# Loading b in long runs, restoring its order in ScalarE's writes, and giving PE whole batches in sequence

## The chip, the cores and the metric

The kernel runs on one core of a Trainium2 chip. The metric is the device time of a run in microseconds (us). PE is the matmul engine (PEld its weight loads), VectorE is DVE in the views, ScalarE is ACT, and SP issues the transfers. "PEclk" is the share of PE's full clock that was granted.

## The reference

```python
batch, m, k, n = 16, 512, 512, 512        # a: [16, 512, 512], b: [16, 512, 512], float32
np.matmul(a, b.transpose(0, 2, 1)).astype(np.float32)
```

Per batch both operands are cast to bf16 and turned by PE (32 transposes of 128 x 128), so that k lies on the partitions in both, as the program's matmuls take them. Then 16 matmuls of 128 x 512 columns make four products of 128 x 512. Two inputs and one output of 1 MB each move per batch, 50.33 MB in all.

## The kernel before

```python
def load(i):
    ...
    nc.sync.dma_start(a_sb[:], a[i].rearrange("(p j) k -> p j k", j=J))    # 8 KB runs
    nc.sync.dma_start(b_sb[:], b[i].rearrange("(o p) k -> p o k", p=P))    # 2 KB runs
def halve(i):
    ...
    nc.scalar.copy(out=a_h[:], in_=a_sb[:])            # ScalarE casts a
    nc.vector.tensor_copy(out=b_h[:], in_=b_sb[:])     # VectorE casts b
def turn(i, ko):                                       # 4 transposes of a, 4 of b, one copy
    ...
    nc.vector.tensor_copy(out=turned[i][:, ko, :], in_=tp[:])
def multiply(i, j):                                    # 4 matmuls, one product copied
    ...
    nc.scalar.copy(out=made[i][:, j, :], in_=ps[:])
...
for i in range(batch):
    for s in range(4):
        multiply(i, s)
        ...
        if i + 1 < batch:
            turn(i + 1, s)
    if i + 2 < batch:
        halve(i + 2)
    ...                                                # store(i), load(i + 5)
```

## Time and profile before

| | kernel before |
|---|---|
| time, median of 3 runs | 131.27 us (130.75 to 131.88) |
| span of the profiled run | 129.7 us |
| DMA engines busy | 97.0% |
| PE, VectorE, ScalarE busy | 74%, 49%, 51% |
| mean granted clock of PE | 0.971 |

The prediction below shows the lines that carry this. Start with the DMA row and the chain's shares: they say whether transfers or engines set the end. Then take single durations from the groups, and the pace of a run of matmuls from the chain, because a matmul's own record holds its latency (392 ns on the mean here, at a pace of 215).

### The profile page before, as it was taken

The page shows a single profiled execution, that of the slowest core. Times are in us where ns is not written, and L with a number is a line of the kernel's source. Part 1 is how long each engine was busy: PE and PEld are TensorE (multiplying, and loading weights), DVE is VectorE, ACT ScalarE, POOL GpSimd, SP SyncE. Part 2 cuts the span into 40 slices and gives each one's busy share as a digit, 9 for nine tenths or more (in the row PEclk, how much of TensorE's full clock was granted, in tenths as well). Part 3 has the DMA queues.
Part 4 walks back from the last instruction along what each step waited for, and adds up shares of the span by engine and source line. Part 5 has one row for each costly group of instructions (what it writes and reads, how often), then busy time and mean ns, then how long its engine had stood idle before and what let it go on. Part 6 is the DMA issues. An engine that isn't in the chain of part 4 may idle for free.

```text
span 129.7 us, 1868 instructions
## 1 busy us (share of the span) xinstructions
PE 95.7 (74%) x768; PEld 55.1 (42%) x768; DVE 63.3 (49%) x80; ACT 66.3 (51%) x81; POOL 0.7 (1%) x6
## 2 busy tenths in 40 slices
PE   0018796969696969687795988879594967969930
PEld 0018363636363636253452545445261634535400
DVE  0026746565656656454655265465545545456200
ACT  3225248483838383827454174756447381283530
POOL 2000000000000000000000000000000000000000
PEclk9999999999999999999999599999999997799998
DMA  3999999999999999999999999999999999999592
GB/s 114 361 427 382 405 423 388 414 403 433 385 428 403 420 415 393 433 367 429 410 420 425 400 433 397 419 417 415 430 399 426 397 431 414 415 426 384 245 349 80
DMA packets 13497, 50.46 MB, mean 389 GB/s; under 512 B 816, under 2 KB 816, under 8 KB 9520
## 3 DMA queue, kind: packets, MB, share of 16 engines
q1 hardware_dynamic: 13488, 50.33, 97.0%
q8 instruction: 6, 0.10, 0.3%
q14 instruction: 3, 0.02, 0.1%
HBM read 33.55 MB, written 16.78 MB: 388 GB/s over the span
## 4 chain that ended last, share of the span: by engine, by line
DMA 53%; PE 26%; ACT 8%; DVE 5%; issue 3%; SPq 1%; DVEq 0%; ACTq 0%
DMA b_sb<-in_b_dram 53%; PE ps L81 17%; ACT a_h L58 7%; PE tp L71 5%; PE tp L69 4%; DVE b_h L59 4%; DVE ab_T L72 2%; SPq L50 1%; ACT o_sb L85 1%; SPq L51 0%; DVEq L59 0%; ACTq L85 0%
## 5 line engine op out<-in xcount | busy, mean ns | idle before, releaser
L81 PE MATMUL ps<-ab_T 128*128 128x512 bf16 x256 | 70.6, 392 | 2.2
L72 DVE COPY ab_T<-tp 128x1024 bf16<-128x1024 bf16 x64 | 44.3, 692 | 41.9 <-PE tp L71 41.8
L85 ACT COPY o_sb<-ps 128x512 f32<-128x512 f32 x64 | 37.5, 586 | 50.5 <-PE ps L81 50.5
L69 PE MATMUL tp<-ident,a_h 128*128 128x128 bf16 x256 | 26.4, 229 | 19.4 <-ACT a_h L58 19.4
L69 PEld LDWEIGHTS <-a_h 128*128 128x128 bf16 x256 | 19.6, 103 | 35.5 <-ACT a_h L58 23.6
L58 ACT CAST a_h<-a_sb 128x2048 bf16<-128x2048 f32 x16 | 30.4, 1902 | 7.4 <-DMA a_sb<-in_a_dram 7.4
L81 PEld LDWEIGHTS <-ab_T 128*128 128x128 bf16 x256 | 22.9, 100 | 24.7 <-DVE ab_T L72 10.1
L71 PE MATMUL tp<-ident,b_h 128*128 128x128 bf16 x256 | 26.3, 228 | 7.0 <-DVE b_h L59 6.9
L59 DVE CAST b_h<-b_sb 128x2048 bf16<-128x2048 f32 x16 | 19.6, 1224 | 16.1 <-DMA b_sb<-in_b_dram 16.0
L71 PEld LDWEIGHTS <-b_h 128*128 128x128 bf16 x256 | 17.8, 102 | 8.6 <-DVE b_h L59 8.6
L58 ACT ACT_TABLE_LOAD x1 | 1.3, 1283 | 0.7 <-PEq L127 0.7
masks.py:199 POOL TENSOR_SCALAR_AFFINE_SELECT ident<-ident 128x128 bf16<-128x128 bf16 x1 | 0.3, 292 | 0.1
masks.py:197 POOL MEMSET ident<- 128x128 bf16 x1 | 0.2, 205 | 0.3 <-POOLq L127 0.3
L127 POOL MEMSET const-bfloat16-1.0<- 128x1 bf16 x1 | 0.1, 101 | 0.0
L127 POOL MEMSET const-uint8-127<- 128x1 uint8 x1 | 0.1, 101 | 0.0
L127 POOL MEMSET const-float32-0.0<- 128x1 f32 x1 | 0.1, 98 | 0.2 <-issue 0.2
L127 POOL MEMSET const-float32-1.0<- 128x1 f32 x1 | 0.1, 98 | 0.0
## 6 DMA issues: line engine op xcount, KB each, us to landing
a_sb<-in_a_dram SPq DMA_DIRECT2D x16, 1024.0 KB, 16.9
b_sb<-in_b_dram SPq DMA_DIRECT2D x16, 1024.0 KB, 18.8
out_dram<-o_sb SPq DMA_DIRECT2D x15, 1024.0 KB, 17.5
out_dram<-o_sb SPq DMA_DIRECT2D x4, 256.0 KB, 3.8
```

The costliest lines, as they stand in the source:

```text
L50: nc.sync.dma_start(a_sb[:], a[i].rearrange("(p j) k -> p j k", j=J))
L58: nc.scalar.copy(out=a_h[:], in_=a_sb[:])
L59: nc.vector.tensor_copy(out=b_h[:], in_=b_sb[:])
L69: nc.tensor.transpose(tp[:, j * P:(j + 1) * P], a_h[:, j, ko * P:(ko + 1) * P], ident[:])
L71: nc.tensor.transpose(tp[:, M + o * P:M + (o + 1) * P], b_h[:, o, ko * P:(ko + 1) * P], ident[:])
L72: nc.vector.tensor_copy(out=turned[i][:, ko, :], in_=tp[:])
L81: nc.tensor.matmul(ps[:], ab_T[:, ko, j * P:(j + 1) * P], ab_T[:, ko, M:], start=(ko == 0), stop=(ko == KO - 1),)
L85: nc.scalar.copy(out=made[i][:, j, :], in_=ps[:])
L127: nc = _bacc.Bacc("TRN2", target_bir_lowering=False, num_devices=1)
```

## The change

The intent is to read b in 8 KB runs as well as a. A partition then holds four neighbouring rows of b, so a product's columns come out in a permuted order. ScalarE puts them right as it copies a product out: it writes each 4-byte element 16 bytes after the last. In the same change PE takes a batch whole (a's transposes, b's, the matmuls) instead of alternating between two batches, and VectorE casts both operands. Beside these, the pools of the loads go from 5 to 6 buffers, those of the turned operands from 3 to 2, and the last output is stored whole instead of in four parts.

```diff
-        nc.sync.dma_start(b_sb[:], b[i].rearrange("(o p) k -> p o k", p=P))
+        nc.sync.dma_start(b_sb[:], b[i].rearrange("(p j) k -> p j k", j=J))
 ... (cuts: pools, names, the old halve and turn)
+    def turn(src, tag):
+        half = hpool.tile([P, J, K], bf16, tag="h" + tag)
+        nc.vector.tensor_copy(out=half[:], in_=src[:])
+        turned = tpool.tile([P, KO, J * P], bf16, tag="t" + tag)
+        for ko in range(0, KO, 2):
+            tp = tppool.tile([P, 2, J * P], bf16, tag="tp")
+            ... (eight transposes)
+            nc.vector.tensor_copy(out=turned[:, ko:ko + 2, :], in_=tp[:])
 ...
-        nc.scalar.copy(out=made[i][:, j, :], in_=ps[:])
+            nc.scalar.copy(
+                out=o_sb[:, j, :].rearrange("m (p j) -> m j p", j=J),
+                in_=ps[:].rearrange("m (j p) -> m j p", j=J),
+            )
 ...
+            aT = turn(a_sb, "a")
+            bT = turn(b_sb, "b")
+            o_sb = multiply(aT, bT)
+            store(i, o_sb)
```

More of the change, by code (lines that the diff above doesn't have):

```diff
@@ L22 @@
     J = M // P
-    NO = N // P
     KO = K // P
@@ L31 @@
     make_identity(nc, ident)
-    apool = ctx.enter_context(tc.tile_pool(name="a_pool", bufs=5))
-    bpool = ctx.enter_context(tc.tile_pool(name="b_pool", bufs=5))
+    apool = ctx.enter_context(tc.tile_pool(name="a_pool", bufs=6))
+    bpool = ctx.enter_context(tc.tile_pool(name="b_pool", bufs=6))
     hpool = ctx.enter_context(tc.tile_pool(name="h_pool", bufs=2))
-    tpool = ctx.enter_context(tc.tile_pool(name="t_pool", bufs=3))
+    tpool = ctx.enter_context(tc.tile_pool(name="t_pool", bufs=2))
     opool = ctx.enter_context(tc.tile_pool(name="o_pool", bufs=5))
@@ L39 @@
     ppool = ctx.enter_context(tc.tile_pool(name="p_pool", bufs=4, space=bass.MemoryType.PSUM))
-    loaded = {}
-    halved = {}
-    turned = {}
-    made = {}
     def load(i):
         a_sb = apool.tile([P, J, K], f32, tag="a")
-        b_sb = bpool.tile([P, NO, K], f32, tag="b")
+        b_sb = bpool.tile([P, J, K], f32, tag="b")
         nc.sync.dma_start(a_sb[:], a[i].rearrange("(p j) k -> p j k", j=J))
-        nc.sync.dma_start(b_sb[:], b[i].rearrange("(o p) k -> p o k", p=P))
-        loaded[i] = (a_sb, b_sb)
@@ L54, in halve @@
-    def halve(i):
-        a_sb, b_sb = loaded[i]
-        a_h = hpool.tile([P, J, K], bf16, tag="ah")
-        b_h = hpool.tile([P, NO, K], bf16, tag="bh")
-        nc.scalar.copy(out=a_h[:], in_=a_sb[:])
-        nc.vector.tensor_copy(out=b_h[:], in_=b_sb[:])
-        halved[i] = (a_h, b_h)
-    def turn(i, ko):
-        if ko == 0:
-            ab_T = tpool.tile([P, KO, M + N], bf16, tag="t")
-            turned[i] = ab_T
-        a_h, b_h = halved[i]
-        tp = tppool.tile([P, M + N], bf16, tag="tp")
-        for j in range(J):
-            nc.tensor.transpose(tp[:, j * P:(j + 1) * P], a_h[:, j, ko * P:(ko + 1) * P], ident[:])
-        for o in range(NO):
-            nc.tensor.transpose(tp[:, M + o * P:M + (o + 1) * P], b_h[:, o, ko * P:(ko + 1) * P], ident[:])
-        nc.vector.tensor_copy(out=turned[i][:, ko, :], in_=tp[:])
@@ L74, in multiply @@
-    def multiply(i, j):
-        ab_T = turned[i]
-        if j == 0:
-            o_sb = opool.tile([P, J, N], f32, tag="o")
-            made[i] = o_sb
-        ps = ppool.tile([P, N], f32, tag="p")
-        for ko in range(KO):
-            nc.tensor.matmul(
-                ps[:], ab_T[:, ko, j * P:(j + 1) * P], ab_T[:, ko, M:],
-                start=(ko == 0), stop=(ko == KO - 1),
-            )
-        nc.scalar.copy(out=made[i][:, j, :], in_=ps[:])
-    def store(i):
-        nc.sync.dma_start(out[i].rearrange("(p j) n -> p j n", j=J), made[i][:])
@@ L90, in store_part @@
-    def store_part(i, j):
-        nc.sync.dma_start(out[i].rearrange("(p j) n -> p j n", j=J)[:, j, :], made[i][:, j, :])
+        nc.sync.dma_start(b_sb[:], b[i].rearrange("(p j) k -> p j k", j=J))
+        return a_sb, b_sb
+    def turn(src, tag):
[4 more added lines that the diff above has]
+            tp = tppool.tile([P, 2, J * P], bf16, tag="tp")
+            for h in range(2):
+                for j in range(J):
+                    nc.tensor.transpose(
+                        tp[:, h, j * P:(j + 1) * P],
+                        half[:, j, (ko + h) * P:(ko + h + 1) * P],
+                        ident[:],
+                    )
+            nc.vector.tensor_copy(out=turned[:, ko:ko + 2, :], in_=tp[:])
+        return turned
@@ new lines, in multiply @@
+    def multiply(aT, bT):
+        o_sb = opool.tile([P, J, N], f32, tag="o")
+        for j in range(J):
+            ps = ppool.tile([P, N], f32, tag="p")
+            for ko in range(KO):
+                nc.tensor.matmul(
+                    ps[:], aT[:, ko, j * P:(j + 1) * P], bT[:, ko, :],
+                    start=(ko == 0), stop=(ko == KO - 1),
+                )
+            nc.scalar.copy(
+                out=o_sb[:, j, :].rearrange("m (p j) -> m j p", j=J),
+                in_=ps[:].rearrange("m (j p) -> m j p", j=J),
+            )
+        return o_sb
@@ L93, with store @@
+    def store(i, o_sb):
+        nc.sync.dma_start(out[i].rearrange("(p j) n -> p j n", j=J), o_sb[:])
+    loaded = {}
     with tc.manual_schedule():
         for i in range(min(AHEAD, batch)):
-            load(i)
-        halve(0)
-        for s in range(KO):
-            turn(0, s)
-        halve(1)
-        for i in range(batch):
-            for s in range(4):
-                multiply(i, s)
-                if i == batch - 1:
-                    store_part(i, s)
-                if i + 1 < batch:
-                    turn(i + 1, s)
-            if i + 2 < batch:
-                halve(i + 2)
-            if i < batch - 1:
-                store(i)
+            loaded[i] = load(i)
+        for i in range(batch):
+            a_sb, b_sb = loaded.pop(i)
+            aT = turn(a_sb, "a")
+            bT = turn(b_sb, "b")
+            o_sb = multiply(aT, bT)
+            store(i, o_sb)
@@ L111 @@
             if i + AHEAD < batch:
-                load(i + AHEAD)
+                loaded[i + AHEAD] = load(i + AHEAD)
 _INS = ['a', 'b']
```

## The prediction

> **What bounds the kernel now.** I read the page first (shares, slices, queues, chain summary), then the groups, the chain in order of time, and the granted clock over 3.41 us stretches. From the page, the transfer rows:
>
> ```profile
> DMA  3999999999999999999999999999999999999592
> ...
> q1 hardware_dynamic: 13488, 50.33, 97.0%
> ...
> DMA 53%; PE 26%; ACT 8%; DVE 5%; issue 3%; SPq 1%; DVEq 0%; ACTq 0%
> ```
>
> The 16 DMA engines are busy in every slice until the last three, 97% of the span, and transfers are 53% of the chain that ended last. No compute engine is over 74%. So the kernel before is bound by moving 50.33 MB, with little to spare: where the chain is not in DMA it runs on PE at 6.58 us a batch (a's cast ends at 28.18 and again at 34.76), against 3.15 MB / 412 GB/s (mean of 20 to 120 us) = 7.6 us of DMA.
>
> From the groups, the durations that I reuse (busy us, then mean ns of one):
>
> ```profile
> L81 PE MATMUL ps<-ab_T 128*128 128x512 bf16 x256 | 70.6, 392 | 2.2
> L72 DVE COPY ab_T<-tp 128x1024 bf16<-128x1024 bf16 x64 | 44.3, 692 | 41.9 <-PE tp L71 41.8
> L85 ACT COPY o_sb<-ps 128x512 f32<-128x512 f32 x64 | 37.5, 586 | 50.5 <-PE ps L81 50.5
> ...
> L58 ACT CAST a_h<-a_sb 128x2048 bf16<-128x2048 f32 x16 | 30.4, 1902 | 7.4 <-DMA a_sb<-in_a_dram 7.4
> ...
> L59 DVE CAST b_h<-b_sb 128x2048 bf16<-128x2048 f32 x16 | 19.6, 1224 | 16.1 <-DMA b_sb<-in_b_dram 16.0
> ```
>
> The 392 ns of a matmul is pipelined latency; the pace is read from the chain (start, us, what):
>
> ```profile
> 116.03 0.05 issue
> 116.08 0.40 PE tp L69 x4
> 116.47 0.22 PE tp L71 x4
> 116.70 0.86 PE ps L81 x4
> ...
> 120.67 0.70 DVE ab_T L72
> 121.37 0.05 issue
> 121.41 2.99 PE ps L81 x13
> 124.43 0.58 ACT o_sb L85
> ```
>
> Four matmuls cost 0.86 us (0.215 each), four transposes 0.22 (0.40 for the first four after a wait), a hand-over between engines about 0.05. In the kernel before these hand-overs lie beside other work, because PE alternates four matmuls of batch i with eight transposes of batch i+1.
>
> The clock matters too (us, PE busy and count, PEld, DVE, ACT, POOL, PEclk, DMA share, GB/s):
>
> ```profile
> 9.62:13.03 3.41, 2.93 (x28) 2.94 (x29) 2.38 (x4) 1.70 (x1) 0.00 (x0) 1.00 0.99 383
> ...
> 67.64:71.06 3.42, 1.69 (x13) 0.77 (x13) 1.78 (x3) 2.03 (x2) 0.00 (x0) 1.00 1.02 432
> 71.06:74.47 3.41, 3.41 (x16) 1.76 (x15) 1.13 (x2) 0.58 (x1) 0.00 (x0) 0.50 1.01 393
> 98.36:101.78 3.42, 1.83 (x17) 1.06 (x17) 1.92 (x2) 1.42 (x3) 0.00 (x0) 1.00 1.01 422
> 105.19:108.60 3.41, 1.60 (x13) 0.76 (x12) 1.69 (x3) 2.08 (x2) 0.00 (x0) 1.00 1.01 425
> 108.60:112.02 3.42, 3.42 (x16) 1.77 (x14) 1.27 (x2) 0.58 (x1) 0.00 (x0) 0.50 1.01 398
> ```
>
> A stretch with too little PE work is followed by one at half clock. Counting by starts, 67.64 holds 4 matmuls and 8 transposes (3072 columns), 105.19 holds 3 and 8 (2560): both are followed by half clock. 98.36 holds 4 and 12 (3584 columns) and is not. At 2.4 columns per ns the limit lies between 1.28 and 1.49 us of column time in 3.41 us; I take 1.4.
>
> [...] the stretch from 9.62 holds 28 transposes and no matmul, and full clock was granted at its end (the 1.00 printed for that stretch itself precedes the first clock record). [...] the trace's busy slices show 367 to 433. [...]
>
> **The change part by part.**
>
> *b in 8 KB runs.* The packet records have 309 ns for 8192 bytes and 84 ns (median) for 2048. Per 8 KB that saves 4 x 84 - 309 = 27 ns; 2048 such runs over 16 engines give 3.5 us in all. It is a gain only while DMA binds.
>
> *Casts.* ScalarE loses 16 x 1.90 = 30.4 us; VectorE gains 16 x 1.22 = 19.6 us, 83 us in all, 5.2 per batch. Neither total exceeds the DMA's.
>
> *Stepped writes.* 64 copies of 586 ns or more. ScalarE has only these, 2.34 us a batch; at twice the duration 4.7. Hidden until the end.
>
> *Sequence.* This is the part that costs. The instruction order of the changed kernel shows: VectorE takes cast a, two copies, cast b, two copies; PE takes 16 transposes of a, 16 of b, 16 matmuls; matmuls 1 and 2 wait for b's first copy, matmul 3 for b's second. The two engines now hand work to each other within one batch. Let T be the end of b's second copy of a batch. Warm, to the next T:
> - 0.05, then the 14 remaining matmuls: 14 x 0.215 + about 0.15 to drain = 3.15. VectorE's cast of the next a (1.22) lies beside them, since its a landed long ago.
> - 8 transposes of the next a, 0.45, and 0.04 to VectorE: its first copy starts at T + 3.7.
> - two copies then cast b: starts 0.61 apart (a cast follows a copy 114.08 to 114.69 in the timeline), so 1.22, and the cast's 1.22: T + 6.15.
> - 0.05 + 8 transposes of b (0.40 + 0.22) + 0.03: b's first copy at T + 6.85.
> - second copy 0.61 later, 0.69 long: T + 8.15. The two early matmuls (0.43) lie beside it.
>
> Sum 8.2 us a batch, all on the path, against 7.4 for DMA with the new runs (7.6 less 3.5/16). DMA goes off the path and five batches of prefetch hide it.
>
> *Clock.* From T + 3.1 to T + 7.6 PE has only 32 transposes, 1.8 us of columns in two lumps (3.1 to 4.0, 6.2 to 7.1). A window that starts at T + x holds under 1.4 us of work for x from about 2.6 to 4.9 (x = 4.0: 0.9; x = 2.6: 0.45 of matmul + 0.9). That is 2.3 of 3.4 phases. The next window is then at half clock and falls mostly on the next batch's matmuls: loss about half of what it covers, 1.0 us for x up to 3.5, 1.3 at 4, 1.55 at 4.5, 1.7 at 4.9. The phase moves on by 3 x 3.41 - 8.2 - loss: x = 3.75 (loss 1.15) gives 4.65 (1.6), then 5.1, which is 1.7 on the grid and harmless (8.2), then 3.75 again. Periods 9.35, 9.8, 8.2: mean 9.1.
>
> *Start and end.* a lands at 5.5 as before. Cast to 6.8; at the cold 0.107 per transpose, as at 10.4 to 12.5, first copy 7.9, second to 9.4, b's cast to 10.6, transposes, copies, T = 13.2. The first period keeps about 1.5 us of cold clock: 9.7. Then 14 x 9.1 = 127.4, last T at 150.3. Last matmuls 3.2 + 0.6 for the clock, last copy 0.6 (0.5 more if stepped writes are slow and queue up), then one 1 MB store instead of four parts already flowing: 4.8 to land (as the first load of a, alone) and about 1.4 around it, 6.2. Span 161.4. Run times exceed the profiled span by about 1.7 (131.5 against 129.7 here): 163; rounded down for the overlaps I may have missed, 162.
>
> **The rivals.**
> 1. *The serial path without the clock's loss.* 13.2 + 9.7 + 14 x 8.2 + 10.5 + 1.7 = 150. For it: only two throttled windows in the kernel before, and the limit is bracketed by few windows. Against: its gaps without matmuls came with late b loads only; here there is a gap of 4.5 us in every batch.
> 2. *DMA stays the bound and gains.* About 131 - 3.5 = 127.5. It needs PE and VectorE to overlap across batches; the order of instructions on both forbids it. I give it 2%.
> 3. *Stepped writes bind.* If a copy took over 2.2 us (3.8 times), ScalarE's four would exceed the period: at 2.5 us, 10 a batch and about 175. [...] nothing here suggests four times; at twice, only the tail sees it.
>
> **Range and chances.** Rival 1 and missed overlaps set the low end, 151; a more frequent half clock or slow writes the high end, 171. Even rival 1 is 14% slower, so slower has 0.97, within 2% 0.015, faster 0.015.
>
> **What would show each step.** DMA share clearly under 90% with gaps, and a chain made of PE and VectorE, with hardly any DMA after the first load. Period 8.2 between b's last copies in undisturbed batches; VectorE waiting about 2.5 us a batch for a's transposes behind the matmuls. Granted clock 0.8 to 0.9, half-clock stretches of 3.41 us in about two batches of three. ScalarE's copy at 586 ns if stepping is free. I am wrong if PE begins a's transposes before the matmuls, if full clock holds throughout (then 150), or if waits name ScalarE or transfers.

The sum stands at 13.2 (first T) + 9.7 (first period) + 14 x 9.1 = 150.3, and 11.1 to the end make a span of 161.4; 1.7 beyond the span give 163, put down as 162. Three inputs are my estimates. The limit of 1.4 us lies between the 3072 and the 3584 columns counted in the trace of the kernel before, at its pace of four matmuls of 512 columns in 0.86 us. The 0.15 us to drain rests on its 2.99 us for 13 matmuls, 0.19 above that pace. That a stepped copy takes up to twice as long was assumed: the kernel before writes nothing in steps, so its trace had no figure.

## The result, and the profile after

The changed kernel takes 161.01 us (160.76 to 161.76, 4 runs), beside 131.57 for the kernel before over the same four rounds: 1.226 times as long, 95% interval 1.218 to 1.234. Every ratio here is the mean time of one kernel's fast runs over the mean of the other's in the same rounds, so it is not quite the ratio of the medians quoted beside it.

The page of the changed kernel: granted clock, DMA share, queue and the chain's shares.

```profile
PEclk9999968969995987999597799969689987969997
DMA  5999999999999999999979979997976060410506
...
q1 hardware_dynamic: 6912, 50.33, 79.0%
...
PE 57%; DVE 30%; issue 3%; DMA 3%; ACT 2%; ACTq 1%; DVEq 0%
```

The same bytes take half as many packets and the engines that move them are busy 79% of a longer span instead of 97%. Gaps open from the middle on. DMA has left the chain (53% before, 3% now, which is the first load); PE and VectorE make 87% of it. The clock dips all along: the trace has ten half-clock records of 3.41 us and a closing one, where the kernel before has two and a closing one.

The groups of the changed kernel (busy us, mean ns, idle before and its releaser):

```profile
L77 ACT COPY o_sb<-ps 128x512 f32<-128x512 f32 x64 | 63.5, 1099 | 89.7 <-PE ps L72 49.6
L72 PE MATMUL ps<-turned 128*128 128x512 bf16 x242 | 74.0, 455 | 6.6 <-DVE turned L64 5.5
L64 DVE COPY turned<-tp 128x1024 bf16<-128x1024 bf16 x64 | 41.4, 686 | 67.2 <-PE tp L59 67.2
...
L53 DVE CAST half<-a_sb 128x2048 bf16<-128x2048 f32 x16 | 19.5, 1217 | 5.8 <-DMA a_sb<-in_a_dram 5.8
L53 DVE CAST half<-b_sb 128x2048 bf16<-128x2048 f32 x16 | 19.5, 1216 | 0.0
```

A stepped product copy takes 1099 ns where the contiguous one took 586, and ScalarE is still idle for 89.7 us. VectorE's work is what was reckoned, but it waits 67.2 us for transposes. Only the first cast of all waited for a transfer.

One batch at full clock, in the chain of the changed kernel (start us, us, what):

```profile
40.17 0.70 DVE turned L64
40.87 0.05 issue
40.92 1.40 PE ps L72 x5
42.32 0.05 issue
42.37 2.32 PE ps L72 x10
44.69 0.46 PE tp L59 x8
45.18 0.48 DVE turned L64
45.66 0.08 issue
45.79 0.68 DVE turned L64
46.47 1.15 DVE half L53
47.61 0.05 issue
47.66 0.63 PE tp L59 x8
48.31 0.70 DVE turned L64
```

Read it as a relay: b's first copy, the matmuls, eight transposes of the next a, two copies, the cast of the next b, eight transposes of it, and b's first copy again, 48.31 - 40.17 = 8.14 us later. Nothing in it overlaps with anything else in it. Over the run the copies that end a batch (b's second) lie 9.58, 9.76, 8.15, 9.48, 9.72, 8.14, ... us apart.

The clock's records in this trace and in that of the kernel before are at 0.50 or 1.00 alone; all but the closing ones last 3.41 us or a multiple of it (6.83, 13.65 here) and follow one another without a gap. In stretches of that grid, changed kernel (us, PE busy and count, PEld, DVE, ACT, POOL, PEclk, DMA share, GB/s):

```profile
28.23:31.64 3.41, 1.55 (x18) 1.10 (x19) 2.70 (x5) 0.00 (x0) 0.00 (x0) 1.00 1.00 423
31.64:35.05 3.41, 3.19 (x8) 1.13 (x8) 1.19 (x2) 1.61 (x2) 0.00 (x0) 0.50 1.02 418
...
38.47:41.88 3.41, 2.03 (x20) 1.30 (x21) 2.69 (x4) 0.00 (x0) 0.00 (x0) 1.00 1.01 418
...
45.29:48.71 3.42, 1.35 (x22) 1.02 (x19) 2.71 (x4) 0.68 (x1) 0.00 (x0) 1.00 1.02 419
48.71:52.12 3.41, 3.07 (x8) 1.11 (x9) 2.02 (x3) 1.07 (x1) 0.00 (x0) 0.50 1.01 423
```

By starts, the stretch from 28.23 holds 2 matmuls and 16 transposes (3072 columns): the next one is at half clock and gets through 8 matmuls. The stretch from 38.47 holds 4 and 16 (4096 columns) and is followed by full clock. In the stretch from 45.29 only transposes start, and half clock follows again. Two batches in three pay. Over both traces, each full-clock stretch with 3072 columns or fewer is followed by half clock (12 with PE work, and one empty stretch after PE's last work in each), and none with 3584 or more is. (This trace lacks 14 of the 256 matmul records; run 4 below has the same order and all records, and its matching stretches hold 2 and 16, then 8, 4 and 16, and no matmul with 18 transposes.)

### The profile page after: what moved, and what is told of

Its sections match the earlier page's. It is cut to its first block, busy times and chain, and to the rows that moved or that the text cites. A ratio compares the mean times of both kernels' runs of the same rounds, so it can differ in the third digit from the quotient of the medians.

```text
span 160.0 us, 1885 instructions
## 1 busy us (share of the span) xinstructions
PE 107.3 (67%) x754; PEld 59.0 (37%) x768; DVE 77.8 (49%) x96; ACT 64.8 (41%) x65; POOL 0.7 (0%) x6
## 4 chain that ended last, share of the span: by engine, by line
PE 57%; DVE 30%; issue 3%; DMA 3%; ACT 2%; ACTq 1%; DVEq 0%
PE ps L72 45%; DVE turned L64 18%; PE tp L59 13%; DVE half L53 12%; DMA a_sb<-in_a_dram 3%; ACT o_sb L77 2%; ACTq L123 1%; DVEq L64 0%; ACTq L77 0%
## 5 line engine op out<-in xcount | busy, mean ns | idle before, releaser
L77 ACT COPY o_sb<-ps 128x512 f32<-128x512 f32 x64 | 63.5, 1099 | 89.7 <-PE ps L72 49.6
L72 PE MATMUL ps<-turned 128*128 128x512 bf16 x242 | 74.0, 455 | 6.6 <-DVE turned L64 5.5
L64 DVE COPY turned<-tp 128x1024 bf16<-128x1024 bf16 x64 | 41.4, 686 | 67.2 <-PE tp L59 67.2
L59 PE MATMUL tp<-ident,half 128*128 128x128 bf16 x512 | 35.6, 225 | 40.1 <-DVE half L53 40.0
L59 PEld LDWEIGHTS <-half 128*128 128x128 bf16 x512 | 31.3, 101 | 46.4 <-DVE half L53 42.8
L72 PEld LDWEIGHTS <-turned 128*128 128x128 bf16 x256 | 27.7, 113 | 48.1 <-issue 24.6
L53 DVE CAST half<-a_sb 128x2048 bf16<-128x2048 f32 x16 | 19.5, 1217 | 5.8 <-DMA a_sb<-in_a_dram 5.8
L53 DVE CAST half<-b_sb 128x2048 bf16<-128x2048 f32 x16 | 19.5, 1216 | 0.0
```

Source lines behind the costliest of these rows:

```text
L53: nc.vector.tensor_copy(out=half[:], in_=src[:])
L59: nc.tensor.transpose(tp[:, h, j * P:(j + 1) * P], half[:, j, (ko + h) * P:(ko + h + 1) * P], ident[:],)
L64: nc.vector.tensor_copy(out=turned[:, ko:ko + 2, :], in_=tp[:])
L72: nc.tensor.matmul(ps[:], aT[:, ko, j * P:(j + 1) * P], bT[:, ko, :], start=(ko == 0), stop=(ko == KO - 1),)
L77: nc.scalar.copy(out=o_sb[:, j, :].rearrange("m (p j) -> m j p", j=J), in_=ps[:].rearrange("m (j p) -> m j p", j=J),)
```

## The experiments

My theory: the loss is the order. One batch's work is handed back and forth between PE and VectorE with nothing beside it (8.14 us a batch, above the time of its transfers, 7.37 in run 3), and the gap this leaves on PE halves its clock. The rivals: the stepped writes, VectorE's added casts, or the path alone without the clock. All results were correct. The medians are over all runs of a kernel.

| run | what | median us | ratio to before | clock |
|---|---|---|---|---|
| - | changed kernel | 161.01 | 1.226 | 0.887 |
| 1 | old order, rest of the change | 141.54 | 1.081 | 0.932 |
| 2 | changed, unread matmuls in the gap | 147.03 | 1.123 | 0.987 |
| 3 | changed, both casts first | 126.76 | 0.968 | 0.984 |
| 4 | changed, 2 KB runs, contiguous writes | 160.74 | 1.228 | 0.888 |
| 5 | changed, ScalarE casts a | 222.45 | 1.698 | 0.781 |
| 6 | before, 8 KB runs, stepped writes | 128.97 | 0.980 | 0.983 |
| 7 | run 1, casts spread over the batch | 129.15 | 0.983 | 0.972 |
| 8 | run 3, 2 KB runs, contiguous writes | 130.22 | 0.991 | 0.964 |
| 9 | run 1, unread matmuls in the gaps | 134.41 | 1.029 | 0.993 |
| 10 | run 3, shorter end | 127.01 | 0.973 | 0.991 |
| 11 | run 3 again, beside run 10 | 126.69 | 0.971 | 0.991 |

Runs 1 to 4, 5 to 8 and 9 to 11 were made on one chip each. The kernel before had medians of 130.89, 131.90 and 130.40 us there.

**Run 4: order and casts without the long runs and the steps.**

```diff
-        nc.sync.dma_start(b_sb[:], b[i].rearrange("(p j) k -> p j k", j=J))
+        nc.sync.dma_start(b_sb[:], b[i].rearrange("(o p) k -> p o k", p=P))
-            nc.scalar.copy(out=<stepped view of o_sb>, in_=<ps, split the same way>)
+            nc.scalar.copy(out=o_sb[:, j, :], in_=ps[:])
```

> The order and the casts of the changed kernel alone: b loaded in 2 KB runs as before, ScalarE's writes contiguous. My theory (runs and stepped writes are off the path): periods as in the changed kernel, 9.2 us on the mean; only the tail is shorter, since the last four copies no longer queue up (1.1 us each down to 0.59): 159 us (157.5 to 160.5). Rival (stepped writes hold something in every batch): under 155 us. Rival (8 KB runs help now): over 161 us.

Measured: 160.74 us, a ratio of 1.228 where the whole change has 1.226. From its groups:

```profile
L77 ACT COPY o_sb<-ps 128x512 f32<-128x512 f32 x64 | 37.5, 585 | 114.9 <-PE ps L72 114.9
```

ScalarE is back at 585 ns a copy and merely idles longer. Its batches end 9.56, 9.76, 8.15, 9.48, 9.72 us apart, like the changed kernel's. So 8 KB runs and stepped writes together neither help nor hurt in this order; that one gains what the other costs is not tested, but the chain of the changed kernel has no transfer after the first load and ScalarE only at the end. The run ends just above my range of 157.5 to 160.5. Not even the end got shorter by the 2 us that I expected: the last copy comes 3.85 us after the last batch's T, the end of b's second copy (154.34 against 150.49) instead of 4.5 (155.26 against 150.74), and 0.65 us in 160 is within what runs differ by.

**Run 2: the clock alone.**

```diff
 ... (cut: the transposes' PSUM pool goes from four tiles to three, for `idle`)
+        if tag == "a":                      # after a's copies, ahead of b's transposes
+            for f in range(8):
+                nc.tensor.matmul(idle[:], ident[:], half[:, f % J, :], start=True, stop=True)
```

> The changed kernel with eight matmuls of 512 columns that nobody reads, put on PE after a's transposes of each batch (1.7 us in the 2.1 us gap in which PE waits for b's cast); the transposes' PSUM tiles go from four to three to make room. More PE work, same results. My theory (about 1 us a batch is half clock from that gap): mean clock over 0.97, all periods 8.15 us, 147 us (145 to 150). Rival (the loss is the serial path alone, the clock only shows it): 161 us or more, since PE has more to do.

Measured: 147.03 us, 14.0 less than the changed kernel although PE has 128 matmuls more. The clock row and b's first copies in the chain of this run:

```profile
PEclk9999999999999999999999999999999999999995
```

```profile
69.69 0.70 DVE turned L66
...
77.84 0.70 DVE turned L66
...
85.98 0.70 DVE turned L66
```

The copies stand 8.15 and 8.14 us apart, and so does every batch of the run. This splits the loss: 14.0 us are half clock (161.01 - 147.03) and 16.1 remain with the path at full clock (147.03 - 130.89 on that chip). Their sum is 30.1 and not the 29.4 of the result, since chips differ; run 4, on the same chip, gives 13.7 and 16.1 of 29.8. The rival that had the path alone is refuted.

**Run 3: one line moved.** VectorE casts b straight after a; PE's order stays.

```diff
-            aT = turn(a_sb, "a")            # each: cast, transposes, copies
-            bT = turn(b_sb, "b")
+            a_h = cast(a_sb, "a")
+            b_h = cast(b_sb, "b")
+            aT = turn(a_h, "a")
+            bT = turn(b_h, "b")
```

> The changed kernel with one line moved: VectorE casts b straight after a, before a's copies; PE's order is unchanged. Both casts then lie beside the matmuls. My theory: the path of a batch falls to 3.7 + four copies 0.61 apart = 6.2 us, under DMA's 7.4, so DMA binds again: 130 us (127 to 135), clock mostly full. Rival (whole batches in sequence on PE must expose PE's time whatever VectorE does): 150 us or more.

Measured: 126.76 us, 34 less than the changed kernel and 3.2% under the kernel before. Its page:

```profile
DMA  3999999999999999999999999999999999999945
...
q1 hardware_dynamic: 6912, 50.33, 96.3%
...
DMA 80%; issue 7%; DVE 3%; SPq 3%; ACT 2%; ACTq 1%; DVEq 0%
```

Four copies of an early batch in a row, and of a late one, from its timeline:

```profile
21.99 2.48 DVE L66 COPY turned<-tp 128x1024 bf16<-128x1024 bf16 x4 [1.45 <-PE tp L61]
28.19 2.48 DVE L66 COPY turned<-tp 128x1024 bf16<-128x1024 bf16 x4 [1.45 <-PE tp L61]
...
76.81 2.48 DVE L66 COPY turned<-tp 128x1024 bf16<-128x1024 bf16 x4
84.18 2.48 DVE L66 COPY turned<-tp 128x1024 bf16<-128x1024 bf16 x4
```

DMA binds again. Batches end 6.20 us apart while the first loads are already there (6.2 was the sum), and 7.37 apart from the eighth on, the pace of 3.146 MB at 427 GB/s (the trace has 425 from 57.20 to 116.13). So whole batches in sequence on PE are not the trouble in themselves: b's cast between a's copies and b's transposes is. With it moved beside the matmuls, PE's gap closes as well and the mean clock is 0.984.

**Run 1: the old order with the rest of the change.**

```diff
 (kernel before, with b in 8 KB runs and stepped writes)
-        nc.scalar.copy(out=a_h[:], in_=a_sb[:])
+        nc.vector.tensor_copy(out=a_h[:], in_=a_sb[:])
```

> Undoes the sequence alone: the order of the kernel before (four matmuls of a batch, then eight transposes of the next), with b in 8 KB runs, stepped writes and both casts on VectorE kept. My theory (the order of PE and VectorE makes the loss): back near the kernel before, 131 us (128 to 134); DMA share back over 93%, mean clock over 0.95. VectorE's two casts stand one after the other at the end of a batch, 1.2 us more on its way to the next transposes than with ScalarE's help, about 7.7 us a batch, so I expect no gain over before. Rival (the stepped writes or VectorE's casts make the loss): 145 us or more. Rival (the 8 KB runs gain 3.5 us as soon as DMA binds): 128 us.

Measured: 141.54 us, a miss by 10.5. Two stretches and two pieces of the timeline from this run:

```profile
60.16:63.57 3.41, 1.79 (x13) 0.76 (x12) 2.96 (x3) 1.72 (x2) 0.00 (x0) 1.00 1.02 430
63.57:66.99 3.42, 3.42 (x15) 1.76 (x14) 1.38 (x2) 1.07 (x1) 0.00 (x0) 0.50 1.03 431
```

```profile
62.04 0.40 PE L69 MATMUL tp<-ident,a_h 128*128 128x128 bf16 x4 [0.74 <-DVE a_h L58]
...
63.17 0.40 PE L71 MATMUL tp<-ident,b_h 128*128 128x128 bf16 x4 [0.74 <-DVE b_h L59]
```

Undisturbed batches take 7.38 us (I had reckoned 7.7), but PE now waits 0.74 us for each of two casts in a row, and those two short waits leave 3072 columns in a stretch. Five of the fifteen intervals are 9.05 instead of 7.38, 1.67 us each, 8.4 in all. I had left the clock out of this estimate.

**Run 9: is that miss the clock?** Six unread matmuls a batch on PE in the two gaps of run 1.

> The kernel in the old order with both casts at the end of a batch (141.5 us, against 131 expected), with six unread matmuls of 512 columns on PE per batch: three ahead of a's first transposes and three between these and b's, in the gaps of about 0.74 us each in which PE waits for the casts. Theory for that miss (undisturbed batches take 7.38 us there as I had reckoned, but the gap also drew half clock in every second or third batch, 1.67 us each, which I had left out): clock over 0.97, 132.5 us (130.5 to 135). Rival (VectorE's two casts cost more than I reckoned by themselves): 138 us or more.

Measured: 134.41 us, clock 0.993, every interval from the second on 7.38. The clock explains 7.1 of the 10.5 us (141.54 - 134.41, on two chips). The remaining 3.4 above my 131 I put down to the path's own 7.38 us, which is no faster than the transfers, so nothing is won while the first loads are ahead; no run parts it further.

**Run 7: the same order, the casts spread.**

```diff
-            if i + 2 < batch:
-                halve(i + 2)                    # both casts after the batch's last step
+                if i + 2 < batch and s in (1, 2):
+                    halve(i + 2, s - 1)         # one cast after each of the two middle steps
```

> The order of the kernel before with 8 KB runs, stepped writes and both casts on VectorE (the kernel that took 141.5 us), and the two casts for batch i + 2 put after the second and third step of batch i instead of both at its end. My theory (there the casts stood at the end of the batch, on PE's way to the next transposes, and the resulting gap also halved the clock): PE's round falls from 7.4 to about 6.4 us, DMA binds: 127.5 us (125 to 131), clock over 0.96. Rival (VectorE's total work holds the interleaved order back): 138 us or more.

Measured: 129.15 us (ratio 0.983, interval 0.973 to 0.992). The same work on the same engines is some 12 us faster in another place (141.54 and 129.15 are from two chips; the ratios, 1.081 and 0.983, say the same). Early batches take 6.40 us, later ones mostly 7.36 to 7.38. Why it stays behind run 3, I have not settled; its clock row still dips in two places, to 0.6 of full clock in a slice, where that of run 11, the repeat of run 3, dips in its last slice only.

**Run 5: the casts undone alone.** ScalarE casts a again, inside the new order.

> The changed kernel with the cast of a back on ScalarE, which undoes the casts alone. My theory (what counts is where an operation stands in its engine's order): ScalarE casts the next a only after this batch's four products, at about T + 4.6 (T is the end of b's second copy), 1.9 us long, so a's first copy moves from T + 3.7 to T + 7.1 and a batch takes 11.6 us warm, some 12.5 with half clock: 205 us (190 to 220), although VectorE has 20 us less to do. Rival (VectorE's added work is what costs): under 158 us.

Measured: 222.45 us, over my range. From the timeline of this run:

```profile
106.86 2.88 ACT L80 COPY o_sb<-ps 128x512 f32<-128x512 f32 x3 [0.63 <-PE ps L75]
109.53 1.91 ACT L54 CAST half<-a_sb 128x2048 bf16<-128x2048 f32 x1
...
111.50 1.07 PE L62 MATMUL tp<-ident,half 128*128 128x128 bf16 x16 [2.95 <-ACT half L54]
```

ScalarE can cast the next a only behind this batch's four products, and PE waits for it. Batches take 12.07 to 13.57 us, 13.0 on the mean, where I had 12.5. In this order, then, giving the cast to VectorE saves some 60 us. That the casts' work is not the cause in itself is shown by run 3, which keeps both on VectorE. Three things lengthen the run together here, the later cast, the slower copies that it stands behind (1085 ns against 586 before) and the lower clock (0.781), and this run does not part them.

**Run 6: long runs and steps on the kernel before.**

> The kernel before with b in 8 KB runs and stepped writes alone; its order and its casts are kept. My theory: copies of 1.08 us instead of 0.59 delay ScalarE's cast of the next a by 0.5 us, so PE's own round goes from 6.58 to 7.1 us, still under DMA's 7.4, and DMA has 3.5 us less to do: 128.5 us (126.5 to 131). Rival (stepped writes cost nothing and gain nothing either, DMA's rate is the same): 131 us. Rival (stepped writes are on the way to the casts by more than that): over 133 us.

Measured: 128.97 us; ratio 0.980, interval 0.970 to 0.990. The profiled run was slow, so I read nothing from its trace. Where DMA binds, this part of the change is worth about 2%, which straddles the limit of a clear gain.

**Run 8: run length where DMA binds.** Run 3 with the edit of run 4.

> The kernel with both casts first (126.8 us) with b in 2 KB runs and contiguous writes. My theory (8 KB runs spare 27 ns per 8 KB, 3.5 us in all where DMA binds, and the shorter tail of contiguous copies gives back about 0.8): 129.5 us (128 to 131), DMA share over 95%. Rival (run length is worth nothing): 126 us.

Measured: 130.22 us. Its queue row against that of run 3 above:

```profile
q1 hardware_dynamic: 13056, 50.33, 98.0%
```

Twice the packets, and a ratio of 0.991 (0.983 to 0.999) where run 3 has 0.968 (0.962 to 0.974) and run 11 has 0.971. The difference of 2.1 to 2.4% is about 3 us, close to the 3.5 reckoned from 309 ns and 84 ns a packet less a shorter end. The packets' time itself (share times span) is 126.1 us here and 120.8 in run 3, 5.3 us less, so the longer runs can cover the gain; but run 8 also has two half-clock stretches (from 64.94 and 88.84) that run 3 has not, and no run parts these.

**Runs 10 and 11: a shorter end for the fastest version.** In the last batch VectorE copies every second product and each quarter is stored by itself.

> The fastest kernel so far (both casts first, 126.8 us) with a shorter end: in the last batch VectorE makes every second copy of a product, and each quarter of the last output is stored as soon as it is copied. My theory (ScalarE's four stepped copies of about 1 us end 0.7 us after the products, and the last store has 1 MB to move alone): 125.3 us (124.3 to 126.3). Rival (the end is set by the last store's fixed time, whatever its size): 126.3 us or more.

> The kernel with both casts first once more, on the chip of the run with the shorter end, to compare them: 126.8 us (126.2 to 127.4).

Measured: 127.01 us, and 126.69 for run 3 repeated beside it. No gain; the rival holds. From the groups and the issues of run 10:

```profile
L80 DVE COPY o_sb<-ps 128x512 f32<-128x512 f32 x2 | 2.1, 1066 | 2.2 <-issue 1.6 <-PE ps L74 0.6
```

```profile
out_dram<-o_sb SPq DMA_DIRECT2D x4, 256.0 KB, 4.6
```

VectorE's stepped copy takes about as long as ScalarE's (1066 ns against 1129 in this run), so the last copy ends at 119.81 instead of 120.03. A quarter needs 4.6 us to land and the last one 4.3, while the last 1 MB store needed 4.0 in run 11 and 3.9 in the changed kernel: the size of the last store hardly mattered here. Run 3 is the version to keep.

## Why the prediction was right

It said 162 us (151 to 171); 161.01 was measured. Point by point:

- **DMA leaves the path.** Right: 79.0% busy, 3% of the chain. In the order of the change the long runs are worth nothing (run 4).
- **The relay of a batch, 8.2 us.** Right: 8.14 (run 2, every batch). The wait named as its sign, VectorE behind the matmuls for a's transposes, is 2.58 us in the undisturbed batch shown above.
- **b's cast on the path.** Right, and shown by run 3: moving it beside the matmuls takes the path to 6.20.
- **Half clock in two batches of three, 9.35, 9.8, 8.2.** Right: 9.47, 9.71, 8.14 repeat to the end. Over the 14 later batches the mean is 128.6 / 14 = 9.19 against 9.1. My estimate of the limit, 1.4 us of columns, sorted these stretches rightly: 3072 columns (1.28 us) drew half clock, 4096 did not. The 2.4 columns per ns behind it are the chain's four matmuls of 512 columns in 0.86 us.
- **Start.** The first T came at 13.47 against 13.2. The first period was mis-sized: 9.7 reckoned, 8.65 measured. The 1.5 us of cold clock fit full clock arriving at 16.44, on the grid of the kernel before (the prediction does not name the time); here the first record of full clock starts 14.57 us from the start, in the kernel before at 13.03. The cold pace in the forecast is that of 16 transposes in 1.70 us there (10.50 to 12.20). Where the grid lies was luck, as far as these two traces show.
- **End.** Mis-sized: 11.1 us reckoned from the last T to the end, 159.96 - 150.74 = 9.2 measured. The last batch met no half clock, and the last store took less than the 6.2 us given it: the span ended 4.7 us after the last copy.
- **Sum.** These two terms were together 2.9 us too long, the 14 periods and the first T 1.5 us too short. The sum of 163 is partly luck in its last digits; the two large terms, path and clock, are not (16.1 and 14.0 us, run 2).
- **Rivals.** The path without the clock gave 150: run 2 makes that case real and gets 147. A faster DMA-bound kernel at 127.5 was ruled out by the order; with the order of VectorE mended it is what run 3 shows, at 126.76. The stepped writes: 1.1 us a copy, 1.9 times, off the path as reckoned for twice.
- **A slip of reading.** The busy slices of the kernel before, the last three left out, show 361 to 433 GB/s, not 367 to 433; nothing rests on it.

## What to carry to other kernels

Two engines that hand one batch to each other, each taking its work in program order as here, add up, however idle each looks (8.14 us a batch here, with PE busy 67% and VectorE 49%); look at where an instruction stands in its engine's order before moving work to another engine. Here one line moved (the second cast ahead of the first copies) turned a kernel 23% slower than before into one 3% faster. And count the columns that PE gets in each stretch of its clock's grid (3072 or fewer in 3.41 us were followed by half clock in the two kernels' traces): short gaps in every batch cost nearly as much here (14.0 us) as the longer path itself (16.1).

## What the traces measured beside the forecast

- Two short waits were enough for half clock in run 1: the stretch of 3.41 us from 60.16, with two waits of 0.74 us and 3072 columns (1.28 us of work at the full pace), was followed by it. The fewest columns that kept full clock in the traces of the two kernels are 3584, in the kernel before from 98.36.
- Transposes were enough for full clock in the kernel before: the stretch from 9.62, with 28 transposes and no matmul (3584 columns), was followed by the trace's first record of it.
- Copying 128 x 512 fp32 from PSUM in 16-byte steps took ScalarE 1099 ns against 586 contiguous, and VectorE 1066 ns (no run has its contiguous time).
- A packet of 8192 bytes took 309 ns and one of 2048 bytes 84 in the kernel before (medians; the means are 313 and 88). Four short ones less one long one are 27 ns, and where DMA bound the longer runs came with about 3 us of 130 (runs 3 and 8).
